# The output product of a two-branch block in seven block products instead of eight

## The chip, the cores and the metric

The kernel runs on one core of one Trainium2 chip. The metric is the device time of one execution in microseconds (us); three runs of the kernel before gave 1612.53, 1613.65 and 1614.66, median 1613.65. A core has a matrix engine (TensorE, in the rows PE, its weight loads PEld), a vector engine (VectorE, DVE), an activation engine (ScalarE, ACT), GpSimd (POOL) and SyncE (SP), which only issues transfers here. Each engine works through its own list of instructions in order and waits on semaphores for the others.

## The reference, cut to what matters

```
proj   = rms_norm(x) @ w_in                      # 2048 -> 12368, 528 tokens (16 meta + 512)
y_a    = sparse_attention(proj ...) * silu(z_a)  # 1024 wide
y_b    = gated_recurrence(proj ...) * silu(z_b)  # 1024 wide
p      = einsum('btnc,ncd->btnd', [y_a, y_b], w_branch)   # 1024 -> 2048 each
g      = sigmoid(gates)                          # 2 x 2048 columns of proj
merged = sum(g * p, axis=2)                      # 512 tokens x 2048
out    = x + merged @ w_out                      # 2048 x 2048
```

All of it is float32. The change is about the last two lines: how `merged` is prepared and how `merged @ w_out` is multiplied.

## The kernel before

Every product runs as three matmuls on float32r operands: each operand is split into a rounded high part and a low part (the rest), and high x high, high x low and low x high are added up in PSUM. A split of a weight block is one ACT copy (L98, `wh<-raw`) and one DVE subtraction (L104, `wl<-raw,wh`) over 128x1024 elements; three pairs of such buffers are there (`NWS`), so the split for block k+3 can only begin when the matmuls of block k are through. Weight blocks arrive by DMA from SP into six `raw` buffers.

The program runs in this order: the columns of `w_in` that the attention and the recurrence need; then the 4096 gate columns; then the branch products with `w_branch` (32 jobs of 128 output columns, 16 per branch, `pg<-yH,wh` and so on); then the output product (four columns of 512). A planner in the kernel (`Core.at`, `pump`) keeps an estimated clock for each engine; side work stands in generators (`spawn`), and `pump()` emits their next instructions after each matmul triple, if the estimated DVE and ACT clocks aren't too far ahead. What it emits when is fixed at build time.

The gate columns are already multiplied in Strassen's form (`run_pair`, table `SEVEN`): a pair of 128-column blocks and two halves of K and two halves of the tokens form a 2x2 block product, done in seven products of 24 matmuls with 256 moving columns instead of eight. It needs four sums of weight blocks (`sum_1` to `sum_4`, DVE, 128x1024 each) and six sums of token blocks, made once. The sigmoid of the gates goes to DRAM (`gd`) and is read back, one 128x512 piece per branch job, two jobs ahead (`load_gate`).

In a branch job (`d_br`), DVE multiplies the PSUM bank by the gate; in the second branch it also adds the first branch's piece, and `split_m` splits the merged piece of 128 features x 512 tokens into `mH` and `mL`.

The output product (L1390 to L1413) takes merged tokens as the stationary operand (128 tokens at a time, four banks) and `w_out` as the moving one, 512 columns wide: 4 columns x 16 K tiles x 4 token tiles x 3 = 768 matmuls. When a column is through, DVE adds x to each bank (`xr<-xr,po`), and SP stores it. x is loaded into `xr` from ACT's queue.

Of the kernel before, what the change touches and what calls it, by code (L numbers as in the profile page):

```python
# [16 lines left out]
D = 2048  # L17
# [157 lines left out]
def hybrid_kernel(ctx, tc, x, meta, vecs, w_in, rows, w_branch, w_out,  # L175
# [133 lines left out]
    class Job:  # L309
        def __init__(self, kind, c0, nc_, meta=False, mv=None, kts=KT, done=None, req=None, n=0, pre=None):  # L310
# [3 lines left out]
            step = 2 if kind == "out" else 8  # L314
# [8 lines left out]
    class Pair:  # L323


        kind, meta = "pair", False

        def __init__(self, c0, done, pre=None):
            self.c0, self.done, self.pre, self.req = c0, done, pre, None
            self.raw = {}  # L330
            for nm, c, k0 in (("11", c0, 0), ("21", c0 + 128, 0), ("22", c0 + 128, 8), ("12", c0, 8)):
                ch = self.raw[nm] = {"job": self, "k0": k0, "nk": 8, "c0": c, "ncols": 128, "i": len(stream)}
                stream.append(ch)
# [11 lines left out]
    def load_chunk(ch):  # L345
# [3 lines left out]
        src = w_branch[0, j.n] if j.kind == "br" else w_out[0] if j.kind == "out" else w_in2  # L349
# [47 lines left out]
    def sum_1(pr):  # L397
        if not hasattr(pr, "s1"):
            load_upto(pr.raw["22"]["i"])
            pr.s1 = wp.tile([128, 1024], F32, name=f"s1_{pr.c0}", tag="s1")  # L400
            E.tt(pr.s1, pr.raw["21"]["raw"], pr.raw["22"]["raw"], OP.add)

    def sum_2(pr):
        if not hasattr(pr, "s2"):
            pr.s2 = wp.tile([128, 1024], F32, name=f"s2_{pr.c0}", tag="s2")
# [12 lines left out]
    def prep_op(k, op):  # L418
# [12 lines left out]
        op["h"] = [h[:, 128 * i:128 * i + 128] for i in range(8)]  # L431
        op["l"] = [l[:, 128 * i:128 * i + 128] for i in range(8)]
        done = {"s3": 2, "22": 3, "s4": 4}.get(nm)
        if done:
            load_upto(first + done - 1 + NRAW)
# [712 lines left out]
    def run_pair(pr, nxt, late):  # L1148

        bk, W = {}, slice(0, 256)  # L1150
        last = nxt is None
# [59 lines left out]

    gd = [[tc.dram_tile([128, 512], F32, name=f"gd{n}_{j}") for j in range(16)] for n in range(2)]
    gate = {}

    def load_gate(n, j):
        g = gate[n, j] = slot("gate")
        nc.sync.dma_start(g[:, :512], gd[n][j])

    merged, mH, mL = {}, {}, {}
# [16 lines left out]
    def split_m(j):  # L1236
        mH[j], mL[j] = slot("mH", F32R), slot("mL", F32R)
        E.act(mH[j][:, :512], merged[j][:, :512], AF.Copy)
        E.tt(mL[j][:, :512], merged[j][:, :512], mH[j][:, :512].bitcast(F32), OP.subtract)
        S.put(merged[j])  # L1240

    def d_br(n, j):
        def f(b):
            g = gate[n, j]
            if n == 0:
                E.tt(g[:, :512], b, g[:, :512], OP.mult)
                merged[j] = g
            else:
                E.tt(g[:, :512], b, g[:, :512], OP.mult)
                E.tt(merged[j][:, :512], merged[j][:, :512], g[:, :512], OP.add)  # L1250
                S.put(g)
                split_m(j)
# [255 lines left out]
```

## Time and profile before

| | |
|---|---|
| runs | 1612.53, 1613.65, 1614.66 us; median 1613.65 |
| profiled execution | 1613.03 us, span 1611.2 us, clock 1.0 |
| PE busy | 1595.2 us (99% of the span) |
| DVE busy | 964.2 us (60%) |
| ACT busy | 552.7 us (34%) |
| POOL busy | 41.8 us (3%) |
| DMA | 175.67 MB |

The chain that ended last is PE for 97% of the span. The branch products run from 1255 to 1429 us, the output product from 1429 to 1607 us. A PE row's duration is longer than its share of the time, since matmuls overlap: the time of a stretch is read from the chain of waits, whose pieces lie end to end, and not from the mean of one matmul.

### The profile page before, as it was taken

The page shows a single profiled execution, that of the slowest core. Times are in us where ns is not written, and L with a number is a line of the kernel's source. Part 1 is how long each engine was busy: PE and PEld are TensorE (multiplying, and loading weights), DVE is VectorE, ACT ScalarE, POOL GpSimd, SP SyncE. Part 2 cuts the span into 40 slices and gives each one's busy share as a digit, 9 for nine tenths or more (in the row PEclk, how much of TensorE's full clock was granted, in tenths as well). Part 3 has the DMA queues.
Part 4 walks back from the last instruction along what each step waited for, and adds up shares of the span by engine and source line. Part 5 has one row for each costly group of instructions (what it writes and reads, how often), then busy time and mean ns, then how long its engine had stood idle before and what let it go on. Part 6 is the DMA issues. An engine that isn't in the chain of part 4 may idle for free.

```text
span 1611.2 us, 26784 instructions
## 1 busy us (share of the span) xinstructions
PE 1595.2 (99%) x11176; PEld 1411.9 (88%) x11176; DVE 964.2 (60%) x1704; ACT 552.7 (34%) x866; POOL 41.8 (3%) x44
## 2 busy tenths in 40 slices
PE   7999999999999999999999999999999999999998
PEld 6888889988889888888888899999999788888887
DVE  6687898436665555454445887777776534542221
ACT  5555322334444222222222344444444322321211
POOL 3100000000000000000000000000000000000000
PEclk9999999999999999999999999999999999999999
DMA  9222333332222232222223344444445844444440
GB/s 252 79 79 79 85 105 85 87 89 73 69 79 67 73 80 66 80 76 70 74 72 99 101 120 134 136 133 131 132 132 166 252 150 131 145 130 151 144 131 27
DMA packets 265594, 175.67 MB, mean 109 GB/s; under 512 B 8644, under 2 KB 238544, under 8 KB 265472
## 3 DMA queue, kind: packets, MB, share of 16 engines
q1 hardware_dynamic: 261952, 167.58, 36.8%
q10 hardware_dynamic: 3456, 6.29, 1.2%
q8 instruction: 87, 1.43, 0.4%
q14 instruction: 35, 0.29, 0.1%
q0 software_dynamic: 64, 0.08, 0.0%
HBM read 157.16 MB, written 16.78 MB: 108 GB/s over the span
## 4 chain that ended last, share of the span: by engine, by line
PE 97%; DMA 1%; DVE 1%; issue 1%; ACT 1%; POOL 0%; SPq 0%; DVEq 0%; ACTq 0%; POOLq 0%
PE pg L90 56%; PE po L90 11%; PE px L88 6%; PE py L88 6%; PE pz L88 5%; PE pw L88 3%; PE phl L90 1%; PE psc L90 1%; PE pov L88 1%; PE plg L90 1%; PE pho L90 1%; PE ppt L94 1%; PE phs L90 1%; PE px L94 1%; PE phd L90 0%
## 5 line engine op out<-in xcount | busy, mean ns | idle before, releaser
L104 DVE TENSOR_TENSOR wl<-raw,wh 128x1024 fp32r<-128x1024 f32 x268 | 328.1, 1224 | 313.6 <-ACT wh L98 313.1
L90 PE MATMUL pg<-hH,wh 128*128 128x264 f32 (+1 forms) x1392 | 478.7, 344 | 0.0
L98 ACT ACTIVATE wh<-raw 128x1024 fp32r<-128x1024 f32 x270 | 285.5, 1057 | 525.8 <-PE pg L90 242.2
L90 PE MATMUL pg<-hH,wl 128*128 128x264 f32 (+1 forms) x1392 | 464.1, 333 | 0.0
L90 PE MATMUL pg<-hL,wh 128*128 128x264 f32 (+1 forms) x1392 | 462.7, 332 | 0.0
L90 PEld LDWEIGHTS pg<-hH,wl 128*128 128x128 f32 x1392 | 261.6, 188 | 26.4
L90 PEld LDWEIGHTS pg<-hH,wh 128*128 128x128 f32 x1392 | 261.7, 188 | 21.7
L90 PEld LDWEIGHTS pg<-hL,wh 128*128 128x128 f32 x1392 | 262.2, 188 | 21.0
L90 PE MATMUL pg<-yL,wh 128*128 128x512 f32 x256 | 100.8, 394 | 0.7 <-DVE yL L104 0.7
L90 PE MATMUL pg<-yH,wh 128*128 128x512 f32 x256 | 100.8, 394 | 0.4 <-ACT yH L98 0.4
L90 PE MATMUL pg<-yH,wl 128*128 128x512 f32 x256 | 101.0, 394 | 0.0
L90 PE MATMUL po<-wh,mH 128*128 128x512 f32 x256 | 100.8, 394 | 0.0
L90 PE MATMUL po<-wl,mH 128*128 128x512 f32 x256 | 100.8, 394 | 0.0
L90 PE MATMUL po<-wh,mL 128*128 128x512 f32 x256 | 100.8, 394 | 0.0
L88 PE MATMUL px<-hL,wh 128*128 128x256 f32 x256 | 72.4, 283 | 0.0
L88 PE MATMUL px<-hH,wl 128*128 128x256 f32 x256 | 72.0, 281 | 0.0
L88 PE MATMUL px<-hH,wh 128*128 128x256 f32 x256 | 71.8, 280 | 0.0
L104 DVE TENSOR_TENSOR gate<-pg,gate 128x512 f32<-128x512 f32 x32 | 22.1, 691 | 70.5 <-PE pg L90 63.9
L90 PEld LDWEIGHTS pg<-yL,wh 128*128 128x128 f32 x256 | 48.1, 188 | 12.8 <-DVE yL L104 1.4
L90 PEld LDWEIGHTS pg<-yH,wh 128*128 128x128 f32 x256 | 48.0, 188 | 12.0 <-ACT yH L98 0.8
L90 PEld LDWEIGHTS po<-wh,mL 128*128 128x128 f32 x256 | 48.1, 188 | 11.2
L90 PEld LDWEIGHTS po<-wh,mH 128*128 128x128 f32 x256 | 48.1, 188 | 11.2
(298 smaller groups left out, 2600.7 us busy)
## 6 DMA issues: line engine op xcount, KB each, us to landing
raw<-in_w_in_dram SPq DMA_DIRECT2D x192, 512.0 KB, 3.9
raw<-in_w_branch_dram SPq DMA_DIRECT2D x32, 512.0 KB, 4.3
raw<-in_w_out_dram SPq DMA_DIRECT2D x32, 512.0 KB, 3.9
gd<-gate SPq DMA_DIRECT2D x32, 256.0 KB, 4.1
gate<-gd SPq DMA_DIRECT2D x32, 256.0 KB, 4.4
x<-in_x_dram SPq DMA_DIRECT2D x16, 256.0 KB, 5.6
xr<-in_x_dram ACTq DMA_DIRECT2D x16, 256.0 KB, 3.8
out_dram<-xr SPq DMA_DIRECT2D x16, 256.0 KB, 4.9
```

Source lines behind the costliest of these rows:

```text
L88: self.nc.tensor.matmul(out, lhsT, rhs, start=start, stop=stop, skip_group_check=True)
L90: self.nc.tensor.matmul(out, lhsT, rhs, start=start, stop=stop)
L94: self.nc.tensor.transpose(out, in_, ident)
L98: self.nc.scalar.activation(out, in_, f, **kw)
L104: self.nc.vector.tensor_tensor(out, a, b, op=op)
```

## The change

The output product is done in Strassen's form too. The blocks are two halves of the tokens, two halves of K (2048 = 2 x 1024) and two halves of a column of 512 (256 each). The tokens remain stationary, 128 at a time, and a weight block of 4 K tiles x 256 columns moves; K is taken in two rounds of 4 + 4 tiles, so that a block is one `raw` buffer. The seven products of a column have a PSUM bank each, open over both rounds. After the second round DVE combines the banks; ACT copies the first product out, and POOL adds it and two other sums to x (`xq`), which is loaded by quarters. The very last product is done one token half after the other, and its halves are added and stored apart.

The merged pieces are prepared by `m_task`, one for features k and k+8: four sums of 128x256 and seven splits (six of them two to an instruction) instead of two splits of 128x512. For that the branch jobs come in the order 0, 8, 1, 9, ... Gates are read back two at a time, in buffers that the weight sums `s1` and `s2` use in the other stages; the first branch's result has a buffer of its own (`mg`).

```diff
-            step = 2 if kind == "out" else 8
+            step = 8
...
+        def __init__(self, kind, c0, c1, k0, k1, nk, ncols, n=0, done=None, more=()):
...
-            for nm, c, k0 in (("11", c0, 0), ("21", c0 + 128, 0), ("22", c0 + 128, 8), ("12", c0, 8)):
+            for nm, c, k in (("11", c0, k0), ("21", c1, k0), ("22", c1, k1), ("12", c0, k1)):
...
+    def load_xq(c):
+        for i in range(2):
+            for j in range(2):
+                q = XQ[c, i, j] = slot("xq")
+                nc.scalar.dma_start(q[:, :512].rearrange("p (b n) -> p b n", b=2), quarter(x, c, i, j))
...
+    def run_out(pr, nxt):
+        c, r, al = pr.c0, pr.n, slice(0, 512)
+        if r == 0:
+            for k in range(4):
+                finish(m_tasks[k])
+        else:
+            for t in m_tasks:
+                finish(t)
+            if nxt:
+                load_xq(nxt.c0)
+        q = lambda i, j: XQ[c, i, j][:, al]
+        for i, (wn, tn, _, _) in enumerate(SEVEN):
+            op = pr.ops[i]
+            split_upto(op["prep"] + 2)
+            if i == 2:
+                od["go"] = True
+            ends = nxt is None and i == 6
+            for tb, kk in [(tb, kk) for tb in range(2) for kk in range(4)] if ends else \
+                    [(tb, kk) for kk in range(4) for tb in range(2)]:
+                o = OB[i][:, 256 * tb:256 * tb + 256]
+                th, tl = (a[:, 128 * tb:128 * tb + 128] for a in TM[4 * r + kk][tn])
+                a, z = r == kk == tb == 0, r == 1 and kk == 3
+                E.mm(o, th, op["h"][kk], a, False, loose=True)
+                E.mm(o, th, op["l"][kk], False, False, loose=True)
+                E.mm(o, tl, op["h"][kk], False, z, loose=True)
+                if ends and kk == 3:
+                    hv = slice(256 * tb, 256 * tb + 256)
+                    E.tt(q(0, 1)[:, hv], q(0, 1)[:, hv], o, OP.add)
+                    nc.sync.dma_start(out[0, 256 + 128 * tb:384 + 128 * tb, c:c + 256], q(0, 1)[:, hv])
+                pump()
+            b = OB[i]
+            if r == 1 and not ends:
+                if i == 0:
+                    p1 = od["p1"] = slot("op")
+                elif i == 1:
+                    d = od["d"] = slot("op")
+                    E.tt(d[:, al], od["p1"][:, al], b, OP.subtract)
+                elif i == 2:
+                    E.tt(q(0, 0), q(0, 0), b, OP.add)
+                    store_q(c, 0, 0)
+                elif i == 3:
+                    E.tt(od["p1"][:, al], b, od["d"][:, al], OP.subtract)
+                elif i == 4:
+                    E.tt(q(1, 1), q(1, 1), b, OP.subtract)
+                    store_q(c, 1, 1)
+                    E.tt(q(0, 1), q(0, 1), b, OP.add)
...
+            if i == 2:
+                sum_4(pr)
+            elif i > 2 and i < 6 and nxt:
+                (sum_1, sum_2, sum_3)[i - 3](nxt)
+            split_upto(op["prep"] + 3)
+            if r == 1:
+                if i == 0:
+                    E.act(p1[:, al], b, AF.Copy)
+                    E.ptt(q(0, 0), q(0, 0), p1[:, al], OP.add)
+                elif i == 1:
+                    E.ptt(q(0, 1), q(0, 1), d[:, al], OP.add)
+                elif i == 3:
+                    E.ptt(q(1, 1), q(1, 1), od["p1"][:, al], OP.add)
+                    E.ptt(q(1, 0), q(1, 0), od["p1"][:, al], OP.add)
...
+    def load_gates(n, p):
+        if (n, p) == (1, 7):
+            g = slots("gate", 2)
+        else:
+            g = wp.tile([128, 1024], F32, name=f"g{n}_{p}", tag=("s2", "s1")[p % 2])
...
+    def m_task(k):
+        while len(S.free) < 7 + (k > 3) or k > 5 and not od.get("go"):
+            yield WAIT
+        r1, r2 = merged[k], merged[k + 8]
+        lo, hi, al = slice(0, 256), slice(256, 512), slice(0, 512)
+        t, u = slots("mt", 2)
+        E.tt(t[:, lo], r1[:, lo], r1[:, hi], OP.subtract)
+        E.tt(r1[:, hi], r1[:, hi], r2[:, hi], OP.subtract)
+        yield E.tt(t[:, hi], t[:, lo], r2[:, hi], OP.add)
+        e = E.tt(u[:, lo], r2[:, lo], t[:, hi], OP.subtract)
...
+                m_tasks.append(spawn(m_task(j - 8), 5 if j > 13 else 3))
...
-    jobs += [Job("out", 512 * c, 512) for c in range(4)]
+    jobs[-1].pre = lambda: [f(jobs[ji]) for f in (sum_1, sum_2, sum_3)]
+    for c in range(4):
+        jobs += [Pair("out", 512 * c, 512 * c + 256, 4 * r, 8 + 4 * r, 4, 256, n=r) for r in range(2)]
```

**PE, the first matmuls of the output product.** `po` is the bank, `mH`, `mL` and `mh` are merged tokens (stationary), `wh` and `wl` the weights. Before, 512 columns, a bank for each 128 tokens:

```order
L90 MATMUL po_14380<-wh_14298,mH_13786 128x512
L90 MATMUL po_14380<-wl_14299,mH_13786 128x512
L90 MATMUL po_14380<-wh_14298,mL_13787 128x512
L90 MATMUL po_14381<-wh_14298,mH_13786 128x512
L90 MATMUL po_14381<-wl_14299,mH_13786 128x512
L90 MATMUL po_14381<-wh_14298,mL_13787 128x512
```

And now:

```order
L88 MATMUL po_14435<-wh_14369,mh_13867 128x256
L88 MATMUL po_14435<-wl_14370,mh_13867 128x256
L88 MATMUL po_14435<-wh_14369,mh_13868 128x256
L88 MATMUL po_14435<-wh_14369,mh_13867 128x256
L88 MATMUL po_14435<-wl_14370,mh_13867 128x256
L88 MATMUL po_14435<-wh_14369,mh_13868 128x256
```

The same triple, at 256 columns, and the two token tiles of a product lie in the two halves of one bank; 24 such rows make a product, 168 a round.

**DVE, the handover from the branch products to the output product.** Before, from the last two branch jobs on (`gate<-pg,gate` is a branch job's multiplication, `mL` the split of a merged piece, `wl` the split of a weight block):

```order
L104 TENSOR_TENSOR gate_14219<-pg_14297,gate_14219 128x512
L104 TENSOR_TENSOR gate_13615<-gate_13615,gate_14219 128x512
L104 TENSOR_TENSOR mL_14331<-gate_13615,mH_14330 128x512
L104 TENSOR_TENSOR wl_14336<-raw_14109,wh_14335 128x1024
L104 TENSOR_TENSOR gate_14258<-pg_14334,gate_14258 128x512
L104 TENSOR_TENSOR gate_13649<-gate_13649,gate_14258 128x512
L104 TENSOR_TENSOR mL_14368<-gate_13649,mH_14367 128x512
L104 TENSOR_TENSOR wl_14387<-raw_14148,wh_14386 128x1024
L104 TENSOR_TENSOR wl_14417<-raw_14187,wh_14416 128x1024
```

Now, from the last branch job's multiplication on (`mt` are sums of token blocks, `sum` and the sum into `raw` those of weight blocks):

```order
L104 TENSOR_TENSOR gate_14278<-pg_14404,gate_14278 128x512
L104 TENSOR_TENSOR mg_13756<-mg_13756,gate_14278 128x512
L104 TENSOR_TENSOR wl_14451<-raw_14238,wh_14450 128x1024
L104 TENSOR_TENSOR wl_14479<-raw_14148,wh_14478 128x1024
L104 TENSOR_TENSOR wl_14511<-sum_226_14399,wh_14510 128x1024
L104 TENSOR_TENSOR mt_14517<-mg_13654 128x256
L104 TENSOR_TENSOR mg_13654<-mg_13654,mg_13687 128x256
L104 TENSOR_TENSOR mt_14517<-mt_14517,mg_13687 128x256
L104 TENSOR_TENSOR mt_14525<-mg_13723 128x256
L104 TENSOR_TENSOR mg_13723<-mg_13723,mg_13756 128x256
L104 TENSOR_TENSOR mt_14525<-mt_14525,mg_13756 128x256
L104 TENSOR_TENSOR mt_14518<-mg_13687,mt_14517 128x256
```

The preparation of the merged pieces 6 and 7 (and 14 and 15) has moved into the first round of the output product, behind the splits for its third to fifth operands; its splits are spread between the splits and sums of the weights that follow.

**DVE, a column's last round.** Before, four additions at the end of a column, between the splits:

```order
L104 TENSOR_TENSOR wl_14597<-raw_14420,wh_14596 128x1024
L104 TENSOR_TENSOR xr_14371<-xr_14371,po_14380 128x512
L104 TENSOR_TENSOR xr_14372<-xr_14372,po_14381 128x512
L104 TENSOR_TENSOR xr_14373<-xr_14373,po_14382 128x512
L104 TENSOR_TENSOR xr_14374<-xr_14374,po_14383 128x512
L104 TENSOR_TENSOR wl_14643<-raw_14450,wh_14642 128x1024
```

Now, in the second round of the first column, from the fourth operand's split on:

```order
L104 TENSOR_TENSOR wl_14740<-raw_14329,wh_14739 128x1024
L104 TENSOR_TENSOR op_14773<-op_14738,po_14436 128x512
L104 TENSOR_TENSOR wl_14776<-sum_230_14585,wh_14775 128x1024
L104 TENSOR_TENSOR xq_14442<-xq_14442,po_14437 128x512
L104 TENSOR_TENSOR raw_14484<-sum_230_14625,raw_14484 128x1024
L104 TENSOR_TENSOR wl_14808<-raw_14482,wh_14807 128x1024
L104 TENSOR_TENSOR op_14738<-po_14438,op_14773 128x512
L104 TENSOR_TENSOR sum_234_14838<-raw_14591,raw_14743 128x1024
L104 TENSOR_TENSOR wl_14841<-raw_14484,wh_14840 128x1024
L104 TENSOR_TENSOR xq_14448<-xq_14448,po_14439 128x512
L104 TENSOR_TENSOR xq_14444<-xq_14444,po_14439 128x512
L104 TENSOR_TENSOR sum_234_14875<-sum_234_14838,raw_14554 128x1024
```

Each product now has, beside its split, a combination of a bank and mostly a sum of weight blocks.

## Rows read from the trace of the kernel before

**Rows 1.** The page: busy us, share of the span and instructions of each engine.

```profile
PE 1595.2 (99%) x11176; PEld 1411.9 (88%) x11176; DVE 964.2 (60%) x1704; ACT 552.7 (34%) x866; POOL 41.8 (3%) x44
```

**Rows 2.** The chain of waits, end of the span: start us, us, what.

```profile
1255.11 173.79 PE pg L90 x749
1428.90 177.93 PE po L90 x768
1606.86 0.69 DVE xr L104
```

**Rows 3.** Windows of three stages: PE, PEld, DVE, ACT, POOL busy; clock; DMA share, GB/s.

```profile
930.00:1238.00 308.00, 308.00 (x2601) 307.84 (x2600) 234.49 (x258) 138.53 (x180) 0.00 (x0) 1.00 0.49 132
1342.00:1428.90 86.90, 86.90 (x376) 70.25 (x375) 49.55 (x60) 23.72 (x30) 0.00 (x0) 1.00 0.42 130
1428.90:1606.80 177.90, 177.90 (x769) 143.97 (x767) 48.61 (x48) 32.46 (x31) 0.00 (x0) 1.00 0.37 118
```

**Rows 4.** The chain of waits in the gate stage; each row one product.

```profile
1010.38 2.85 PE px L88 x24
...
1030.27 2.85 PE px L88 x24
...
1226.36 2.84 PE pz L88 x24
1229.20 2.85 PE px L88 x24
```

**Rows 5.** The page's groups: line, engine, operation; busy us, mean ns.

```profile
L90 PEld LDWEIGHTS po<-wh,mH 128*128 128x128 f32 x256 | 48.1, 188 | 11.2
...
L88 PE MATMUL px<-hH,wh 128*128 128x256 f32 x256 | 71.8, 280 | 0.0
```

**Rows 6.** Timeline of DVE in the gate stage: start us, us, what, idle before.

```profile
1223.55 0.42 DVE L104 TENSOR_TENSOR gate<-p,pz 128x256 f32<-128x256 f32 x1
1223.89 1.22 DVE L104 TENSOR_TENSOR s<-s,raw 128x1024 f32<-128x1024 f32 x1
1225.02 1.22 DVE L104 TENSOR_TENSOR wl<-raw,wh 128x1024 fp32r<-128x1024 f32 x1
1226.40 0.42 DVE L104 TENSOR_TENSOR gate<-p,pw 128x256 f32<-128x256 f32 x1 [0.16 <-PE pw L88]
...
1230.27 1.23 DVE L104 TENSOR_TENSOR wl<-raw,wh 128x1024 fp32r<-128x1024 f32 x1 [0.61 <-ACT wh L98]
```

**Rows 7.** Timeline of ACT, gate stage and output stage.

```profile
1229.17 1.06 ACT L98 ACTIVATE wh<-raw 128x1024 fp32r<-128x1024 f32 x1 [1.78 <-PE pz L88]
1402.54 0.63 ACT L98 ACTIVATE mH<-gate 128x512 fp32r<-128x512 f32 x1 [3.99 <-DVE gate L104]
1430.40 2.70 ACTq L1393 DMA_DIRECT2D xr<-in_x_dram  x4
1467.88 1.78 ACTq L1393 DMA_DIRECT2D xr<-in_x_dram  x4
```

**Rows 8.** Timeline of DVE in the output stage.

```profile
1470.11 1.28 DVE L104 TENSOR_TENSOR xr<-xr,po 128x512 f32<-128x512 f32 x2
```

**Rows 9.** Timeline of POOL and DVE in the first 30 us.

```profile
16.79 1.47 POOL L108 TENSOR_TENSOR el<-raw,eh 128x512 fp32r<-128x512 f32 x1 [2.02 <-ACT eh L98]
17.04 1.50 DVE L114 TENSOR_SCALAR xm<-xm,stm 16x512 f32<-16x512 f32 x1
18.21 1.47 POOL L108 TENSOR_TENSOR el<-raw,eh 128x512 fp32r<-128x512 f32 x1
21.85 0.47 DVE L114 TENSOR_SCALAR xm<-xm,stm 16x512 f32<-16x512 f32 x1
```

**Rows 10.** The page's DMA issues: KB each, us to landing.

```profile
raw<-in_w_in_dram SPq DMA_DIRECT2D x192, 512.0 KB, 3.9
gate<-gd SPq DMA_DIRECT2D x32, 256.0 KB, 4.4
out_dram<-xr SPq DMA_DIRECT2D x16, 256.0 KB, 4.9
```

More of the change, by code (lines that the diff above doesn't have):

```diff
@@ L430, in prep_op @@
         h, l = hi_lo(k, src, 1024)
[L431 to L435, printed above, removed]
+        w = pr.ncols
+        op["h"] = [h[:, w * i:w * i + w] for i in range(pr.nk)]
+        op["l"] = [l[:, w * i:w * i + w] for i in range(pr.nk)]
+        used = {"s3": 2, "22": 3, "s4": 4}.get(nm)
+        if used:
+            load_upto(first + used - 1 + NRAW)
     cvec = cp.tile([128, 35], F32, name="cvec")
@@ L1146, in hybrid_kernel, with run_pair @@
              ("s1", "t1", "z", 0), ("22", "t4", "w", 0), ("s4", "22", "z", 1))
-    def run_pair(pr, nxt, late):
+    def run_pair(pr, nxt, late, last):
         bk, W = {}, slice(0, 256)
-        last = nxt is None
         for i, (wn, tn, bn, on_) in enumerate(SEVEN):
@@ L1210, in run_pair, with quarter, store_q @@
                         next(ysplit, None)
+    OB, XQ, od = [], {}, {}
+    def quarter(t, c, i, j):
+        return t[0, 256 * j:256 * j + 256, c + 256 * i:c + 256 * i + 256].rearrange("(b p) n -> p b n", p=128)
+    def load_xq(c):
[3 more added lines that the diff above has]
+                nc.scalar.dma_start(q[:, :512].rearrange("p (b n) -> p b n", b=2), quarter(x, c, i, j))
+    def store_q(c, i, j):
+        q = XQ[c, i, j]
+        nc.sync.dma_start(quarter(out, c, i, j), q[:, :512].rearrange("p (b n) -> p b n", b=2))
+        S.put(q)
@@ L1212, in hybrid_kernel @@
     gd = [[tc.dram_tile([128, 512], F32, name=f"gd{n}_{j}") for j in range(16)] for n in range(2)]
     gate = {}
[L1215 to L1219, printed above, removed]
+    def load_gates(n, p):
+        if (n, p) == (1, 7):
+            g = slots("gate", 2)
+        else:
+            g = wp.tile([128, 1024], F32, name=f"g{n}_{p}", tag=("s2", "s1")[p % 2])
+            g = [g[:, 0:512], g[:, 512:1024]]
+        for i in range(2):
+            nc.sync.dma_start(g[i][:, :512], gd[n][p + 8 * i])
+            gate[n, p + 8 * i] = g[i]
@@ L1271, in pre_t, with req_br @@
         t_task.append(spawn(tops_task(), 2))
-    def req_br(n, j):
+    def req_br(n, p):
         def f():
-            if j == 0 and n == 1:
-                finish(splits[1])
-            for jj in ((0, 1, 2) if (n, j) == (0, 0) else (j + 2,)):
-                m, i = (n, jj) if jj < 16 else (1, jj - 16)
-                if m < 2 and (m, i) not in gate:
-                    load_gate(m, i)
-            if (n, j) == (0, 4):
+            if p == 0:
+                if n:
+                    finish(splits[1])
+                else:
+                    load_gates(0, 0)
+            if p < 7:
+                load_gates(n, p + 1)
+            elif n == 0:
+                load_gates(1, 0)
+            if (n, p) == (0, 2):
                 yr = load_y(1)
@@ L1373, in hybrid_kernel @@
     npair, late = 0, []
+    first_out = min(i for i, j in enumerate(jobs) if j.kind == "out")
     for ji, job in enumerate(jobs[2:], 3):
@@ L1379, in hybrid_kernel @@
             job.req()
-        if job.kind == "pair":
+        if job.kind == "gate":
             npair += 1
```

99 lines of the change are left out of this document (53 added, 46 removed).

## The prediction

> **What bounds the kernel now.** I read the page's busy shares first: PE is busy for 99% of the span, DVE for 60% [rows 1]. The chain of waits says the same by place: from 1255 us on it is PE without a break, the branch products and then 177.93 us of output product, and behind it only one DVE addition and the last store [rows 2]. So a matmul taken away is worth its slot on PE, as long as what PE waits for still comes in time. The windows show how much room DVE has for that: 234.5 of 308 us busy (76%) in the gate stage, which runs in Strassen's form already, 49.6 of 86.9 (57%) in the second half of the branch stage, 48.6 of 177.9 (27%) in the output stage; PE is at 100% in all three, and its granted clock at 1.00, the 2.4 GHz level [rows 3]. The gate stage is the model for what is to come, and most numbers below are from it.
>
> **The matmuls of the output product.** Removed: 768 of 512 columns, which take 177.93 us, 231.7 ns each [rows 2]. Added: 4 columns x 2 rounds x 7 products x 24 = 1344 of 256 columns, all with 128x128 weights loaded for each, as now. In the gate stage the seven products of a pair, 168 matmuls of the same shape, take 1030.27 - 1010.38 = 19.89 us, 118.4 ns each [rows 4]. 8 such rounds make 159.1 us. Term: -18.8 us. Fewer columns at a lower rate: 7/8 of the columns in 0.894 of the time.
>
> **DVE in the output product.** A product lasts 19.89/7 = 2.84 us. Two DVE rows that follow one another without a wait start 1.13 us apart for 128x1024 and 0.34 for 128x256 [rows 6], and two of 128x512 take 1.28 us, 0.64 each [rows 8]; these are the costs in a full queue, while the rows' own durations (1.22, 0.42, 0.69) are the upper bound. A first round has 7 splits and 4 sums, 12.4 us of 19.9. A second round has 7 combinations of 128x512 more: 16.9 us (upper bound 18.3). Both fit, but an average is not enough: a split for operand k+3 can begin only when product k frees its buffers, and it is due two products later. In the gate stage the ACT copy starts as the product ends (end 1229.20 [rows 4], copy 1229.17 [rows 7]), the DVE split 1.07 us after the end [rows 6] and takes 1.23, so 5.68 - 2.30 = 3.4 us remain. Without POOL, a second round doesn't use them up: behind products 2 to 5 its queue has a combination (two behind product 4), a sum and a split, 2.90, 2.90, 3.54 and 2.90 us against 2.84 a product, so DVE falls 0.9 us behind at most, and a split that stands behind a combination and a sum still ends 0.64 + 1.13 + 1.23 + 0.9 = 3.9 us after its product, 1.8 before it is due. What is behind is made up in the next first round.
>
> **The handover.** Here the order shows two `m_task`s (pieces 6 and 7) in the first round of the output product, since their buffers come free only when the branch products are over. Let the last branch matmul end at 0. DVE then does the last multiplication and addition and the third operand's split, then waits for the end of product 0 and of product 1 (5.68); the fifth operand's split ends at 5.68 + 1.07 + 1.13 = 7.88. From there to the last token split that the second round's second product needs, the queue holds 9 rows of 1024, 6 of 512 and 9 of 256: 9 x 1.13 + 6 x 0.64 + 9 x 0.34 = 17.1 us, so that split ends at 24.95. It is due at that product's fourth K tile: the product starts at 8 x 2.84 = 22.72, the fourth tile 18/24 of a product later, 24.85. So it comes 0.1 us late by the spacing of the rows, and 2.05 late by their own durations. On the way the next round's first split ends at 19.3 where 19.88 is due. Bounds 0.1 and 2.1; I take 0.5, near the spacings, since they are how a full queue runs in this trace.
>
> **x added on POOL.** Four additions of 128x512 in each column, none in the trace at this place. POOL's nearest row took 1.47 us [rows 9], and 4 x 1.47 us is hidden beside 39.8 us of a column unless it holds up DVE. The trace shows that it can: a DVE TENSOR_SCALAR of 16x512 takes 0.47 us alone, and 1.50 when it starts 0.25 us behind a POOL addition; it ends just behind that addition's end [rows 9]. It waited out the other engine. Whether a DVE addition or split with both inputs in SBUF does so too, no row shows. If it doesn't, the term is 0. If it does, I follow the second round's queue with the POOL rows in it (round starts at 0, products and operands counted from 0, product i ends at 2.84(i+1)). ACT first issues four loads of x (1.78 to 2.70 us [rows 7]), then makes operand 3's copy and moves the first product out (0.63 [rows 7]); DVE's split of operand 3 ends near 6.0, the first POOL addition runs to 7.4, operand 4's split waits for it and ends at 8.5, the second addition runs beside the third bank's combination to 9.95, then a sum and a split to 12.2, the fourth bank's combination to 12.85, a sum to 13.98, the third addition to 15.4, the last operand's split to 16.5 (due 17.04), the fourth addition beside the two combinations of bank 4 to 17.95, a sum to 19.1, and the next round's first split to 20.2, where 19.88 is due: 0.35 us late, for three columns (the last has no next) 1.05. With the rows' own durations 1.7 us a column, 5.1 in all. Bounds 0 and 5.1; I take 1.0, by the spacings. A rule speaks against the change here: the Trainium skill, SBUF — State Buffer, section "Who interferes with whom", says that a VectorE instruction with two SBUF inputs contends with a GpSimd instruction that reads SBUF, and that whoever is second waits for the whole instruction. The stretched TENSOR_SCALAR agrees (1.50 against 0.47 us), and no row here shows a two-input one; by the rule the term is the 1.0 to 5.1, without it 0.
>
> **The tail.** The last product is done in halves on one bank, and the order shows PE's second half waiting for DVE. Price: a 256-column row lasts 0.28 us [rows 5] where the next would start after 0.118, so it runs on for 0.16; DVE starts 0.04 behind its end (1226.36 [rows 4], 1226.40 [rows 6]) and takes 0.42, and PE is back about 0.1 later, which no row shows; the bounds below hold 0 to 0.4: 0.7 us. In return the last addition takes 0.42 instead of 0.69 [rows 2], and the last store is half the size; the time of that store's flight is left as it is (out stores land in 4.9 us, median [rows 10]). Term: +0.4, bounds 0 and +1.
>
> **The branch stage.** Two branch jobs are 48 matmuls of 231.7 ns, 11.1 us. Their DVE work was two times a weight split and three rows of 512, 6.1 us, and is now 2 x 1.13 + 7 x 0.64 + 5 x 0.34 = 8.4 us (upper bound 9.4), hidden beside PE; ACT gains 0.6 us copies only. What would be late first is the next weight split, due a job (5.6 us) after it may begin, and before it in any one job stand at most 2.0 us of token work (4 x 0.34 + 0.64). A gate's load now waits until the pair of jobs before it is through; behind it on SP stand two weight loads, due four jobs later. The gate itself is due 3 x 5.56 = 16.7 us after its issue at the earliest and lands in 4.4 us [rows 10]. Weight blocks of `w_out` come in 1 KB runs instead of 2 KB; the gate stage's come in 512 B runs, one each 4.97 us, and land in 3.9 us [rows 10]. Both cost nothing while PE keeps its 100%.
>
> **Sum.** -18.8 + 0.5 + 1.0 + 0.4 = -16.9 us against the profiled execution's 1613.03 (span 1611.2): 1596.1. The median of the runs shown is 0.6 above it, 1613.65, so 1596.8; I say 1597.
>
> **Rivals.**
> *DVE becomes the bound in the second rounds.* For it: 16.9 us of DVE and 4 x 1.47 = 5.9 of POOL are 22.8 in 19.9 us if all exclude one another, and with the rows' own durations 24.2. Against it: seven combinations read PSUM, and a POOL addition can lie beside them. Price: handover 2.1, three columns at 1.7 to 4.3 us (24.2 - 19.9), tail 0.4, so 7.6 to 15.4 us of the 18.8 given back: 1602 to 1610, likeliest 1603. Chance 0.17.
> *POOL and DVE don't meet at all, and the handover is free.* Then only the tail stands against the 18.8 us: 1595. No row shows a two-input instruction held up, so this can be; against it, the one DVE row of 0.47 us that began behind a POOL row was. Chance 0.18.
> *PE's own rate in the output product is the weight load's.* A load of 128x128 tokens takes 188 ns [rows 5]; before, each has a slot of 231.7 ns and need not overlap another. If loads of token slices didn't overlap one another, 1344 x 188 = 252.7 us against 177.93: 1688, slower by 75. It decides from 177.93/1344 = 132.4 ns a matmul. For it: no row has token slices as weights at a faster pace than 231.7. Against it: in the gate stage loads of the same size and duration stand 118.4 ns apart. Chance 0.03.
> *A transfer is late.* A store of x waits on SP for a product and its combination, and loads of `w_out` stand behind it. Price: one landing, 3.9 us, for each of three columns less the slack: the blocks behind the three stores are due at the fourth product of the next round, 11 us after. Only a queue twice as slow gives some us, 1600. Chance 0.05.
>
> **Chances.** My forecast, 1595.5 to 1602 by its terms, 0.57. About 0.2% (3.2 us) is what a measurement can tell from no change. Only the weight-load rival is slower (0.03), and the worst of the first rival ends near no change (0.03): faster 0.94. The range goes from no stall at all, 1613.65 - 18.8 less a us for the runs' spread, 1594, to the handover, the second rounds and the tail at their upper bounds, 2.1 + 5.1 + 1 on top of 1594.85, 1603, and one more for the first rival's lower end: 1604. Left out are most of that rival, the weight loads and half of the late transfer.
>
> **What would show it.** In the chain of waits a round of the output product at 19.9 us, 168 `po` matmuls between rows of the same length as the gate stage's; a break of 0.1 to 2 us in the second round's second product of the first column, put down to DVE's `mh`; breaks of some tenths at the beginning of the next three columns, put down to `wl`; a DVE row of 1024 stretched from 1.22 to as much as 2.6 us beside a POOL addition, or a POOL row stretched beside DVE's; one break of 0.7 us before the last 12 matmuls. The prediction is wrong if the matmuls stand more than 122 ns apart without a wait, if the branch stage's 173.8 us grow, or if POOL costs DVE no time at all while PE still waits.

## The result, and the profile after

The changed kernel takes 1593.43 us (median of 4 runs, 1593.20 to 1595.98), the kernel before on the same chip 1613.68 (1612.53 to 1614.66): a ratio of 0.9878 [0.9861, 0.9895]. Faster, as forecast, by 20.2 us (1.2%) where 16.9 were expected; the time lies 0.6 us below the lower end of the range. The profiled execution took 1593.2 us (span 1591.3) against 1613.03 (1611.2).

The page of the changed kernel, busy time, share of the span and instructions of each engine, answers to [rows 1]: 576 matmuls more, yet 18.6 us less of PE, and PE still at 99%.

```profile
PE 1576.6 (99%) x11752; PEld 1427.3 (90%) x11752; DVE 1059.5 (67%) x1821; ACT 586.7 (37%) x910; POOL 72.2 (5%) x60
```

The same three windows as in [rows 3] (us, then PE, PEld, DVE, ACT and POOL busy, granted clock, DMA share, GB/s). The gate stage is as it was, DVE's work in the second half of the branch stage rose from 49.6 to 64.0 us without PE losing anything, and in the output stage DVE went from 27% to 82% of the window.

```profile
930.00:1238.00 308.00, 308.00 (x2602) 307.91 (x2601) 234.41 (x257) 138.76 (x179) 0.00 (x0) 1.00 0.49 133
1342.00:1428.90 86.90, 86.90 (x381) 70.59 (x380) 63.99 (x97) 28.53 (x40) 0.00 (x0) 1.00 0.42 129
1428.90:1587.00 158.10, 157.40 (x1329) 156.89 (x1328) 129.89 (x129) 62.02 (x66) 30.41 (x16) 1.00 0.43 136
```

The chain of waits at the end (start, us, what), beside [rows 2]. The branch products last 173.81 us, as before (173.79). The output product runs from 1427.66 to 1587.77, 160.11 us against 177.93.

```profile
1253.85 173.81 PE pg L90 x749
1427.66 5.70 PE po L88 x48
...
1452.82 0.04 issue
1452.86 132.71 PE po L88 x1120
...
1585.59 0.43 DVE xq L104
...
1586.07 1.70 PE po L88 x12
...
1587.79 0.42 DVE xq L104
```

The chain is interrupted twice, and a view of what PE waited for from 1342 us on (us in total, times, longest) gives exactly these two: the handover and the tail. At the starts of the later columns, where the forecast had 1.0 us, there is nothing.

```profile
PE po L88 <- DVE xq L104: 0.5, 1, 0.5
PE po L88 <- DVE mh L104: 0.2, 1, 0.2
```

The last stage can be compared without what comes ahead of it: from the first output matmul to the end of the span, 1611.2 - 1428.90 = 182.30 us before and 1591.3 - 1427.66 = 163.64 after. So 18.66 us come from the output product and its tail. The remaining 1.2 us of the two profiles lie at the start: PE's first wait, for the load of the small vectors, is 8.4 us before and 7.3 after, in a part that the change doesn't touch. In the view of PE's waits over the first 40 us, the changed kernel has:

```profile
PE pc L94 <- DMA vrow<-in_vecs_dram: 7.3, 1, 7.3
```

### The profile page after: what moved, and what is told of

Its sections match the earlier page's. It is cut to its first block, busy times and chain, and to the rows that moved or that the text cites. A ratio compares the mean times of both kernels' runs of the same rounds, so it can differ in the third digit from the quotient of the medians.

```text
span 1591.3 us, 28166 instructions
## 1 busy us (share of the span) xinstructions
PE 1576.6 (99%) x11752; PEld 1427.3 (90%) x11752; DVE 1059.5 (67%) x1821; ACT 586.7 (37%) x910; POOL 72.2 (5%) x60
## 4 chain that ended last, share of the span: by engine, by line
PE 96%; DVE 2%; DMA 1%; issue 1%; ACT 1%; POOL 0%; SPq 0%; DVEq 0%; ACTq 0%; POOLq 0%
PE pg L90 57%; PE po L88 9%; PE px L88 6%; PE py L88 6%; PE pz L88 5%; PE pw L88 3%; PE phl L90 1%; PE psc L90 1%; PE pov L88 1%; PE plg L90 1%; PE pho L90 1%; PE ppt L94 1%; PE phs L90 1%; DVE wl L104 1%; PE px L94 1%
## 5 line engine op out<-in xcount | busy, mean ns | idle before, releaser
L104 DVE TENSOR_TENSOR wl<-raw,wh 128x1024 fp32r<-128x1024 f32 x276 | 342.0, 1240 | 212.5 <-ACT wh L98 210.3
L98 ACT ACTIVATE wh<-raw 128x1024 fp32r<-128x1024 f32 x278 | 294.1, 1058 | 491.3 <-PE pg L90 260.1
L88 PE MATMUL po<-wh,mh 128*128 128x256 f32 x896 | 159.3, 281 | 0.7 <-DVE xq L104 0.5
L88 PEld LDWEIGHTS po<-wh,mh 128*128 128x128 f32 x896 | 137.7, 189 | 1.1 <-DVE xq L104 0.7
L88 PE MATMUL po<-wl,mh 128*128 128x256 f32 x448 | 126.1, 281 | 0.0
L88 PEld LDWEIGHTS po<-wl,mh 128*128 128x128 f32 x448 | 84.4, 189 | 0.2
L98 ACT ACTIVATE wh<-sum 128x1024 fp32r<-128x1024 f32 x48 | 50.9, 1061 | 85.4 <-PE pw L88 26.8
L104 DVE TENSOR_TENSOR wl<-sum,wh 128x1024 fp32r<-128x1024 f32 x48 | 61.9, 1289 | 16.6 <-ACT wh L98 16.6
L108 POOL TENSOR_TENSOR xq<-xq,op 128x512 f32<-128x512 f32 x16 | 30.4, 1914 | 689.7 <-ACT op L98 645.5
```

Source lines behind the costliest of these rows:

```text
L88: self.nc.tensor.matmul(out, lhsT, rhs, start=start, stop=stop, skip_group_check=True)
L98: self.nc.scalar.activation(out, in_, f, **kw)
L104: self.nc.vector.tensor_tensor(out, a, b, op=op)
L108: self.nc.gpsimd.tensor_tensor(out, a, b, op=op)
```

## The experiments

Two theories stood at the outset. The first is the forecast's: the gain is the matmuls' slots, POOL and DVE exclude one another, and that costs PE little because it stays hidden. The second: they don't meet at all, and the 1.0 us set down for it was never there. Beside them were the noise of the start, the tail, and the rate of narrow matmuls.

**The kernel before, once more** (no edit).

> The kernel before, unchanged, profiled a second time. In the first profile PE's first matmul waited 8.38 us for the load of the vectors, in the changed kernel's 7.28 us, and the whole program stood 1.0 to 1.1 us earlier from there on. Theory 'start': that load lands at different times from one execution to the next, so 1.1 us of the changed kernel's 19.9 us is luck of the start; then this wait differs from 8.38 us here or lies near 7.3. Rival 'change': the changed program starts faster every time; then this wait is 8.3 to 8.4 us again. In both the output product takes 177.9 us.

1613.29 us. Output product to end of span: 182.32 us, as in the first profile; PE's first wait was 6.5 us, followed by 1.1 us at the next stage. Its chain has the same shape as [rows 2]:

```profile
1255.38 173.80 PE pg L90 x749
1429.18 177.93 PE po L90 x768
...
1607.13 0.69 DVE xr L104
```

**The changed kernel, on two other chips** (no edit).

> The changed kernel, unchanged, a second time. Theory 'start': PE's first wait is anything from 7 to 8.5 us; the time against the kernel before is 18.8 to 20.3 us less, and what remains when the start is left out is 18.6 to 18.9. Rival 'change': the wait is 7.2 to 7.4 us again and the time 19.9 to 20.3 us less. The output product, from its first matmul to its last addition, takes 160.1 us in both.

> The changed kernel, unchanged, beside the others of this call. From the first matmul of the output product to the end 163.6 to 163.7 us, and the time 18.7 us less than before, give or take 1 us of the start.

1593.58 us (1593.28 to 1594.38), ratio 0.9877 [0.9863, 0.9892], and 1593.93 (1593.13 to 1595.15), ratio 0.9877 [0.9860, 0.9893]. From the first output matmul to the end: 163.71 and 163.65 us. So the last stage repeats within 0.1 us, while its start does not: 1427.99 and 1429.45, with first waits of 7.3 and 9.1 us; with the 9.1 falls the rival that the changed program starts faster every time. No edit of this study touches what runs ahead of it: over its 14 profiles the output product begins between 1427.66 and 1430.52 us, and the first profile of the changed kernel is the earliest.

**POOL's additions left out.** Without them four of the terms are missing from the output.

```
-    E.ptt(q(0, 0), q(0, 0), p1[:, al], OP.add)
-    E.ptt(q(0, 1), q(0, 1), d[:, al], OP.add)
-    E.ptt(q(1, 1), q(1, 1), od["p1"][:, al], OP.add)
-    E.ptt(q(1, 0), q(1, 0), od["p1"][:, al], OP.add)
```

> The changed kernel without POOL's 16 additions (the outputs lack those terms). Theory 'hidden': POOL and DVE do wait for each other in the second rounds (DVE rows of 1.22 us became 1.74 and 2.33), but PE never waits for it, so the time is the changed kernel's within 0.4 us and DVE's rows of 1024 are all 1.2 us again. Rival 'DVE': the exclusion cost PE some tenths a column that don't show as waits; then it is 0.7 to 1.5 us faster.

1593.40 us (1592.86 to 1596.78), ratio 0.9880 [0.9865, 0.9895]; the output product on PE takes 159.89 us (160.10 or 160.11 with them, in three profiles). So POOL costs nothing that a whole time could tell, and some 0.2 us in the output product. But it isn't because the engines don't meet. Groups of the output stage (count, busy us, mean ns, idle before), first of the changed kernel:

```profile
L104 DVE TENSOR_TENSOR wl<-raw,wh 128x1024 fp32r<-128x1024 f32 x39 | 52.0, 1335 | 15.5 <-ACT wh L98 15.4
L108 POOL TENSOR_TENSOR xq<-xq,op 128x512 f32<-128x512 f32 x16 | 30.4, 1914 | 689.7 <-ACT op L98 645.5 <-DMA xq<-in_x_dram 26.8 <-issue 9.4
```

and without POOL:

```profile
L104 DVE TENSOR_TENSOR wl<-raw,wh 128x1024 fp32r<-128x1024 f32 x39 | 47.7, 1223 | 19.9 <-ACT wh L98 19.9
```

The same 39 splits lose 4.3 us with POOL beside them, and find it again in their waits for ACT: 15.5 instead of 19.9 us. The timeline of DVE in the second round of the second column shows which ones are held up, and POOL's by whom. DVE, with POOL's additions at work:

```profile
1491.80 1.23 DVE L104 TENSOR_TENSOR wl<-raw,wh 128x1024 fp32r<-128x1024 f32 x1 [1.61 <-ACT wh L98]
...
1494.60 2.11 DVE L104 TENSOR_TENSOR wl<-sum,wh 128x1024 fp32r<-128x1024 f32 x1 [0.35 <-ACT wh L98]
...
1499.49 0.68 DVE L104 TENSOR_TENSOR op<-po,op 128x512 f32<-128x512 f32 x1
1500.09 1.21 DVE L104 TENSOR_TENSOR sum<-raw,raw 128x1024 f32<-128x1024 f32 x1
1501.22 2.31 DVE L104 TENSOR_TENSOR wl<-raw,wh 128x1024 fp32r<-128x1024 f32 x1
1503.46 1.27 DVE L104 TENSOR_TENSOR xq<-xq,po 128x512 f32<-128x512 f32 x2
...
1505.79 1.21 DVE L104 TENSOR_TENSOR wl<-raw,wh 128x1024 fp32r<-128x1024 f32 x1
```

and POOL's timeline there, two additions to a row:

```profile
1492.33 3.29 POOL L108 TENSOR_TENSOR xq<-xq,op 128x512 f32<-128x512 f32 x2 [26.85 <-DMA xq<-in_x_dram]
1500.25 4.45 POOL L108 TENSOR_TENSOR xq<-xq,op 128x512 f32<-128x512 f32 x2 [4.63 <-DVE op L104]
```

DVE's split that starts at 1494.60 lasts to 1496.71, 0.89 us over its 1.22; POOL's first pair ends at 1495.62, 1.1 us ahead of that. The one at 1501.22 is 1.09 us over. And POOL waits in its turn: its second pair starts 0.16 us behind a DVE sum and takes 4.45 us for two additions. The DVE rows that read PSUM (`xq<-xq,po`, 1.27 us for two) and lie beside POOL are not stretched. So what DVE loses in this round is 0.89 + 1.09 = 1.98 us. The round is a typical one: over the stage the splits of raw blocks lose 4.3 us, those of sums 3.1 (22.7 against 19.6 us for 16) and one group of sums 0.4, 7.8 us in four second rounds.

**POOL's additions on DVE instead.**

```
-    E.ptt(...)
+    E.tt(...)      # all four
```

> The changed kernel with the 16 additions on DVE instead of POOL. Each costs DVE about 0.6 us in a full queue, 2.4 us a column; the waiting for POOL costs it 0.5 + 0.5 + 1.1 = 2.1 us a column. Theory 'exclusion': POOL's additions cost DVE about as much time as doing them itself, so the time is the changed kernel's within 0.6 us. Rival 'POOL relieves DVE': DVE's second rounds get 2.4 us longer and, being near their limit, PE loses 1.5 to 2.4 us in each of three columns, 4.5 to 7 us in all.

1593.74 us (1592.98 to 1594.35), ratio 0.9876 [0.9860, 0.9893]: the same. In the groups of this kernel the splits are back at their plain duration, and the additions cost 0.69 us each:

```profile
L104 DVE TENSOR_TENSOR wl<-raw,wh 128x1024 fp32r<-128x1024 f32 x39 | 47.6, 1224 | 16.0 <-ACT wh L98 16.0
L104 DVE TENSOR_TENSOR xq<-xq,op 128x512 f32<-128x512 f32 x16 | 10.6, 686 | 0.0
```

Four in a round are some 2.6 us of DVE, against 1.98 us that POOL's presence takes in the round above: by moving them to POOL the kernel saves almost nothing on DVE. PE loses 0.2 us at one split, and its output product is 160.40 us.

**More work for DVE in the second rounds.** In each second round that has a column behind it, each product gets an addition of 128x512 with both inputs in SBUF, 21 in all, some 4.2 us a round.

```
+    if r == 1 and nxt:
+        ...                                   # a spare buffer, zeroed by DVE before its first use
+        E.tt(od["more"][:, al], od["more"][:, al], od["more"][:, al], OP.add)
```

> The changed kernel with one more DVE addition of 128x512 (a spare buffer to itself) behind each of the seven products of the second rounds, in the three columns that have a next one: 21 of about 0.6 us, 4.2 us a round. Theory 'at the edge': the next round's first split is ready only 0.3 to 0.4 us before its matmul, so with five more additions ahead of it, less the 0.9 us that DVE idles early in the round, it comes some 1.7 us late, the ones behind it more: 2 to 3 us a column, 6 to 9 us in all, as breaks of PE at the beginning of the next rounds put down to wl. Rival 'room': DVE has room left in these rounds and PE loses less than 2 us in all.

1610.26 us (1608.83 to 1611.56), ratio 0.9978 [0.9968, 0.9987]: more than expected. PE's output product grows by 14.9 us, to 174.97. What PE waited for from 1342 us on:

```profile
PE po L88 <- DVE wl L104: 10.8, 9, 2.1
```

and the group of the added rows:

```profile
L104 DVE TENSOR_TENSOR more<-more 128x512 f32<-128x512 f32 x21 | 23.1, 1098 | 0.0
```

The additions average 1.10 us where such a row takes 0.68 alone. The 10.8 us of waits are not the whole 14.9. Each of the nine breaks costs some 0.26 us beyond the wait that the view counts (shown at the tail, below), 2.3 us in all. And behind the last break the granted clock fell (end of this text): the next 323 matmuls in the chain take 39.91 us, where 118.5 ns each would make 38.3, so some 1.5 us. About 0.3 us stay unexplained.

**The same without POOL** (the two edits above together; POOL's terms are missing again).

> The same 21 more DVE additions, but without POOL's 16 (the outputs lack those terms). Theory 'exclusion has a price at the edge': POOL's additions hold DVE up for 2.1 us a round, so without them PE loses 2 us a column less than with them, 0 to 1 us a column, 0 to 3 us in all. Rival 'no price': POOL's additions fall where DVE would idle, and the loss is the same as with them within 1 us.

1595.36 us (1595.26 to 1596.82), ratio 0.9890 [0.9875, 0.9905]; the output product takes 161.90 us. The same 21 additions now cost PE 1.3 us of waits for `wl`, in two places, and their group has the plain duration:

```profile
L104 DVE TENSOR_TENSOR more<-more 128x512 f32<-128x512 f32 x21 | 14.3, 683 | 0.0
```

POOL's additions, worth 0.2 us in the changed kernel, are worth 174.97 - 161.90 = 13.1 us here, 4.4 a column, the fall of the clock among them. The exclusion is real; the changed kernel has just enough room for it.

**The same number of additions, one input in PSUM** (POOL as in the changed kernel; the edit is against the kernel with more work).

```
-        E.tt(od["more"][:, al], od["more"][:, al], od["more"][:, al], OP.add)
+        E.tt(od["more"][:, al], od["more"][:, al], b, OP.add)
```

> The 21 more DVE additions once more, with POOL's additions in place, but now each reads the PSUM bank of its product and the spare buffer, so only one input is from SBUF. DVE's own work is as long as with the additions of the spare buffer to itself, which made the output product 14.9 us longer (1.9 without POOL). Theory 'exclusion between two-input rows': these additions run in 0.68 us beside POOL's instead of 1.10 in the mean, POOL holds up only splits and sums, and PE loses 5 to 9 us. Rival 'the queue is simply too long': it loses 13 to 16 us again.

1600.25 us (1599.84 to 1603.71), ratio 0.9922 [0.9907, 0.9937]; output product 166.36 us, 6.25 more than the changed kernel's, 4.6 of it PE's waits for `wl` in seven breaks. The group of the added rows:

```profile
L104 DVE TENSOR_TENSOR more<-more,po 128x512 f32<-128x512 f32 x21 | 14.3, 681 | 2.6 <-PE po L88 2.4
```

The mean is 681 ns with POOL at work, as without it. In the second column's second round a split and an added row stand beside the same pair of POOL's additions, which runs to 1509.33. DVE:

```profile
1505.86 2.32 DVE L104 TENSOR_TENSOR wl<-raw,wh 128x1024 fp32r<-128x1024 f32 x1
1508.10 0.67 DVE L104 TENSOR_TENSOR more<-more,po 128x512 f32<-128x512 f32 x1
```

and POOL:

```profile
1504.89 4.44 POOL L108 TENSOR_TENSOR xq<-xq,op 128x512 f32<-128x512 f32 x2 [4.11 <-DVE op L104]
```

The split, with two SBUF inputs, is stretched, the added row isn't. So it is the second SBUF input that makes a DVE row wait. That is what the Trainium skill says (SBUF — State Buffer, section "Who interferes with whom"): a VectorE instruction with two SBUF inputs contends with a GpSimd instruction that reads SBUF; one with at most one SBUF input, outside the 2-port modes, doesn't. The trace agrees, with 1098 against 681 ns.

What is left of the loss is not DVE's plain load alone: without POOL the same number of additions cost 161.90 - 159.89 = 2.0 us. Most of the rest goes with POOL's additions, which still hold up the splits: 39 `wl<-raw` take 1333 ns on average here, 1220 without POOL. How much of it is the added rows' own waits for their banks (2.4 us in the line above), no run tells apart.

**The last half product in another bank, two ways.** First the second half of a spare tile, then a bank whose first-round part is added early.

```
+    other = i == 6 and tb == 1 and c == 1536
+    if other: o = OB[7][:, 0:256]
...
+    OB += [wide[:, 0], wide[:, 1]]             # the two banks of the spare tile
```

> The changed kernel with the very last product's second token half in a bank of its own, so that PE need not wait until DVE has read the first half. The changed kernel's trace has PE waiting 0.51 us there. Theory 'bank': that wait goes, the last addition starts 0.5 us earlier and the time is 0.5 us less. Rival 'DVE or stores': the first half's addition and store, which then lie beside the last matmuls, hold up the last ones, and the time stays within 0.2 us.

1595.17 us (1594.02 to 1596.31), ratio 0.9887 [0.9872, 0.9901]. PE's wait of 0.5 us is still there: the program orders the two halves of this tile one behind the other, although they are two banks (in a bank of another tile, next run, the wait goes). The edit failed to take the wait away and tells nothing of its worth.

```
+    o = OB[0][:, 0:256] if ends and r == tb == 1 else ...
...
+    E.tt(q(0, 1)[:, hv], q(0, 1)[:, hv], OB[6][:, hv], OP.add)     # behind product 1, last column
```

> The changed kernel with the last second half of the very last product written to the bank of the first product, which is long free then; what the first round left in its own bank is added by DVE earlier (one more addition of 128x256). With the two halves in two halves of one tile PE still waited 0.5 us. Theory 'bank': now the wait is gone, and from the first matmul of the output product to the end it is 163.2 us instead of 163.7, the time 0.5 us less than the changed kernel's. Rival: the last additions or stores follow one another too closely then, and it stays at 163.6 to 163.8 us.

1594.02 us (1593.06 to 1594.80), ratio 0.9878 [0.9864, 0.9893]. The wait is gone; the chain has one run of matmuls to the end:

```profile
1453.70 134.11 PE po L88 x1132
...
1587.84 0.42 DVE xq L104
```

From the first output matmul to the end it takes 1591.4 - 1428.51 = 162.9 us, 0.75 less than the changed kernel: more than the wait of 0.51, since a break costs more than its wait. In whole times that can't be told from the changed kernel on the same chip (1593.93).

**The last product in one piece.**

```
-    ends = nxt is None and i == 6
+    ends = False
```

> The changed kernel with the last product undivided: one addition of 128x512 and one store of 256 KB behind it. Theory 'tail by its rows': PE's wait of 0.5 us goes, the last addition takes 0.69 instead of 0.42 us and the last store lands in 2.6 us, as the 256 KB ones of the kernel before, instead of 2.0; together 0.3 to 0.4 us slower than the changed kernel, and from PE's last matmul to the end 4.4 us, as before the change, instead of 3.5. Rival 'end is fixed': what follows the last store is as long whatever its size, and the time is 0.2 us less.

1595.53 us (1593.92 to 1596.34), ratio 0.9888 [0.9873, 0.9902]. The wait is gone here too, but the last addition is whole and so is its store: PE ends at 1589.90, the span at 1594.4, 4.5 us behind, where the changed kernel needs 3.53. Its output product began at 1430.52, so start to end is 163.88 us: the halves are worth 0.2 us net, and the profile's larger span (1594.4 against 1591.3) is mostly its late start.

**Narrow matmuls alone.** The kernel before, each 512-column matmul cut in two of 256, weights loaded for each.

```
+    for f in range(2):
+        o, fs = banks[t][:, 256 * f:256 * f + 256], slice(256 * f, 256 * f + 256)
+        E.mm(o, mH[kt][:, ts], ch["h"][i][:, fs], ...)       # and the two others likewise
```

> The kernel before with each 512-column matmul of the output product cut into two of 256 columns, the halves of one bank: 1536 instead of 768, and no Strassen. Theory 'count times 118.4 ns': 1536 x 118.4 = 181.9 us against 177.9, so 4.0 us slower than before; with 1344 the same rate gives the changed kernel's 159.1 us. Rival 'token slices as weights cost more at this pace': above 122 ns a matmul, over 187 us, 9 us slower or more.

1614.93 us (1613.74 to 1617.50), ratio 1.0010 [1.0001, 1.0020]. The output product in its chain:

```profile
1428.05 181.09 PE po L88 x1536
```

117.9 ns each: token slices as weights do follow at that pace, and the loads are no bound. 3.2 us longer than 177.93, where 4.0 were expected.

## Why the prediction was right, and where not

The mechanism that carries the gain, fewer matmuls at the gate stage's rate, was right. What failed in the sum are two small terms: the 1.0 us set down for POOL holding up DVE and the 0.4 us for the tail. They came out as 0.2 and -0.1, and so the output product gained 18.66 us where 16.9 were forecast. That alone puts the changed kernel at 1595.0, still in the range. What took the time below it is the step that gave the range's lower end a single us for the spread of the runs: over the profiles the start of the output product moves by 2.9 us, for reasons ahead of the change, and that the result's profile has the earliest start of all 14 is luck.

**The matmuls: right.** -18.8 us forecast. The run with the last product in one piece has no break at the tail: its output product takes 1589.90 - 1430.52 = 159.38 us. Less the handover's break (0.44) and POOL's 0.22, both below, 158.72 us are left for 1344 matmuls, 118.1 ns each: -19.2. The narrow run's 117.9 ns would make 158.5. The rival of the weight load (75 us slower) fell with it.

**The handover: right, 0.44 us for 0.5.** The view counts 0.18 us of waiting, and a break costs some 0.26 more (see the tail). Two rows of DVE's timeline were forecast. The first is the fifth operand's split, the second the last token splits:

```profile
1434.48 1.23 DVE L104 TENSOR_TENSOR wl<-sum,wh 128x1024 fp32r<-128x1024 f32 x1 [1.56 <-ACT wh L98]
...
1451.18 0.69 DVE L104 TENSOR_TENSOR mh<-mg,mh 128x512 fp32r<-128x512 f32 x1
1451.78 1.36 DVE L104 TENSOR_TENSOR mh<-mt,mh 128x256 fp32r<-128x256 f32 x3
```

The fifth operand's split is done at 1434.48 + 1.13 = 1435.61, 7.95 us behind the last branch matmul (forecast 7.88), and the last token split at 1452.82 in the chain of waits, 25.16 behind it (forecast 24.95, due at 24.85); of the three rows in the last line it is the second, and one of them is 128x512. A queue of 24 rows came out within 0.3 us, on the spacing of the rows, not on their durations. Some 0.2 us of that is luck: the 0.64 us for a row of 512 was half of a pair's duration, and the next row really starts 0.60 behind (1451.18 and 1451.78), while two rows of 256 are followed only after some 0.46 (1435.62 and 1436.08).

**POOL: the mechanism was right, the price was not.** The step that failed is the ledger that ended with the next round's first split "0.35 us late". By its own times it had POOL hold up DVE by about 3 us in a second round; the rows above give 1.98. It charged 1.47 us for each POOL addition; the first one here ends at 1492.33 + 1.86 = 1494.19, only 1.16 behind the DVE split for which it waited (1491.80 + 1.23 = 1493.03). The next column's first split therefore ends at 1505.79 + 1.21 = 1507.00; PE comes to it at about 1507.37 (the 460 matmuls from 1452.86 on, 118.5 ns each): 0.37 early instead of 0.35 late. So PE never waits there, and POOL's additions cost the output product 0.22 us (160.11 against 159.89) and not 1.0, by the one profile without them; a ledger 0.7 us off was enough for that. The rival that POOL and DVE don't meet gave nearly the same time and is refuted all the same.

**The tail: wrong in sign.** Forecast +0.4, bounds 0 to +1. The break was sized rightly: the output product takes 160.11 us with it and 159.38 without (last product in one piece), 0.73 us, against 0.7. The rows of PE there, around the wait of 0.51 us:

```profile
1585.28 0.28 PE L88 MATMUL po<-wh,mh 128*128 128x256 f32 x1
1586.07 0.39 PE L88 MATMUL po<-wh,mh 128*128 128x256 f32 x1 [0.51 <-DVE xq L104]
1586.29 0.28 PE L88 MATMUL po<-wl,mh 128*128 128x256 f32 x1
```

The row before has run on for 0.16 us when the wait begins, and the first matmul behind it stands 0.22 us ahead of the next instead of 0.12: a break costs some 0.26 us beyond its wait. But "the time of that store's flight is left as it is" was wrong: between PE's end and the end of the span lie 3.53 us after and 4.37 before. 0.27 of the 0.84 is the shorter addition; the rest is the last store. The last DMA issue (KB, us to landing), after:

```profile
out_dram<-xq SPq DMA_DIRECT2D x1, 128.0 KB, 1.9
```

before:

```profile
out_dram<-xr SPq DMA_DIRECT2D x1, 256.0 KB, 2.4
```

and with the last product in one piece:

```profile
out_dram<-xq SPq DMA_DIRECT2D x1, 256.0 KB, 2.5
```

So the term is 0.73 - 0.84 = -0.11 us, a tenth below its bounds. No other term left them.

**The branch stage: right.** 173.81 us for 173.79, with 14.4 us more DVE work in the window.

**The sum.** -19.21 + 0.44 + 0.22 - 0.11 = -18.66 us, measured three times within 0.1 (182.30 and 182.32 against 163.64, 163.71, 163.65). By it the changed kernel stands at 1613.65 - 18.66 = 1595.0, inside the range. The medians on three chips gained more, 20.2, 19.3 and 19.0 us. The start of the output product varies by 2.9 us over the profiles for two reasons that lie far ahead of the change. PE's first wait is 6.5 to 9.1 us. And in the three profiles in which it is followed by a break of 1.0 to 1.2 us at the next stage, 0 to 0.6 in the others (the kernel before run again, the whole last product, more work for DVE), the granted clock falls in the first 50 us. Windows of that stretch (us, PE busy, granted clock, DMA share, GB/s), of the changed kernel, whose first wait is 7.3 us:

```profile
0.00:50.00 50.00, 41.78 (x302) 1.00 0.74 204
```

and of the kernel with the last product in one piece, with the same first wait and an output product that begins 2.86 us later:

```profile
0.00:50.00 50.00, 40.72 (x278) 0.93 0.75 204
```

That is enough for the differences between the medians. For the two later chips the runs of both kernels are listed with their clocks: those at 1.00 alone average 1612.3 and 1612.6 us before and 1593.7 and 1593.9 after, 18.6 and 18.8 us less, as the last stage has it. Of all their runs, 8 of the 20 before stand below 1.00, and 1 of the 8 after. For the first chip's 20.2 us no such comparison is on record, and what of it lies beyond 18.66 stays open between the start and chance, since the intervals of the ratios are 4.7 to 5.5 us wide.

**The rival that DVE becomes the bound** stood closer than its time says: 4.2 us more of DVE in a second round turn 0 us into 5 a column beside POOL's additions, and into 0.7 without them.

## What to carry over

Where an engine queue has to be in time for another, work the ledger row by row with the spacing of a full queue; here it came out within 0.3 us over 24 rows, with some luck, and where a ledger ends within 0.4 us of a deadline, as POOL's did, either side of it is open. A vector addition moved to POOL beside DVE rows with two SBUF inputs frees hardly any DVE time (2.0 us lost for 2.6 saved in a round), so it could as well have stayed. Compare a late stage from its own first instruction, not from the start of the span, when what runs ahead of it varies by nearly 3 us.

## What the hardware showed

- DVE `TENSOR_TENSOR` rows with both inputs in SBUF and POOL's rows wait for each other: a 128x1024 split 2.11 and 2.31 us instead of 1.22, POOL's additions 1914 ns on average, their waiting included, where a POOL row took 1.47 us [rows 9]. With one input in PSUM, nothing (681 ns for 683).
- With 21 more additions PE stood still for up to 2.06 us, and then, in one of three places, the granted clock fell. Windows of that run (us, then PE, PEld, DVE, ACT and POOL busy, granted clock, DMA share, GB/s): after breaks of 0.72 and 2.06 us in the third column the clock averages 0.68 for 4 us, between the levels of 1.2 and 2.4 GHz, and 26 matmuls are done, against 103 in the next 12 us at the upper level. Breaks of 0.73 and 2.06 us in the second column (first two rows) and of up to 2.04 in the first left it at 1.00; what makes the difference is open.

```profile
1518.00:1521.00 3.00, 1.45 (x12) 1.45 (x13) 3.00 (x5) 2.01 (x2) 0.00 (x0) 1.00 0.15 52
1521.00:1524.00 3.00, 2.63 (x23) 2.43 (x22) 3.00 (x4) 1.06 (x1) 0.00 (x0) 1.00 0.26 87
1560.00:1564.00 4.00, 1.94 (x14) 1.73 (x13) 4.00 (x6) 1.90 (x2) 0.00 (x0) 0.89 0.40 136
1564.00:1568.00 4.00, 4.00 (x26) 4.00 (x26) 4.00 (x6) 0.37 (x2) 0.00 (x0) 0.68 0.22 70
1568.00:1580.00 12.00, 12.00 (x103) 12.00 (x103) 9.14 (x8) 4.88 (x5) 0.00 (x0) 1.00 0.34 109
```

- The last store of the kernel lands in 1.9 us when it has 128 KB, in 2.4 and 2.5 us when it has 256 KB; 256 KB stores just ahead of it in the changed kernel land in 2.1. The time to landing is no function of the size alone.
